# A residual stream kept feature by feature in a two-layer encoder: output projection and row norms

## The chip, the cores and the metric

One core of a Trainium2 chip runs the whole program in one launch. The metric is the device time of that launch in microseconds. A core has TensorE (matmuls, with its own weight loads), VectorE, ScalarE, GpSimd and SyncE (SP, which here issues all DMAs), and 16 DMA engines between DRAM and the on-chip memories SBUF (128 partitions) and PSUM (where matmuls write).

## The reference, cut to what matters

Two request groups, a prompt of 1024 rows and a sample of 512, go through two layers with the same weights; a row has 1024 features.

```
h = rms_norm(x, norm_g[l])                       # x / sqrt(mean(x^2) + 1e-6) * g, row by row
u = h @ w_in[l]                                  # 1024 x 3840: branches and gate
mkv = rms_norm(mem, mem_norm_g[l]) @ w_mem_kv[l] # 256 memory rows per group
layer 0: short gated conv | sliding-window attention | memory attention
layer 1: axial attention  | differential attention   | memory attention
x = x + (concat(branches) * silu(z)) @ w_out[l]  # 1280 x 1024
```

All is float32. The kernel writes each float32 factor of a large matmul as a high and a low part and adds three products: high x high, high x low, low x high.

## The kernel before, in words

Tokens go in halves of 512 (two for the prompt, `hf` 0 and 1, one for the sample). The projections take the contraction in 128 features at a time; activations for them lie in SBUF with the features on the partitions, in pairs of tiles [128, 2, 512] (ring `act`, 16 tiles). A weight chunk is 256 columns wide and comes in 4 pairs (`load_w`, line 204; 5 for the output projection): a DMA into `wraw`, ScalarE's cast to the high part `whi` (line 186), and a subtraction for the low part `wlo` (line 187) on VectorE or GpSimd in turns. `whi` and `wlo` have 7 tiles each.

`mm_a` (line 301) holds 128 tokens of activations stationary and moves 256 weight columns: the result has tokens on the partitions. `mm_b` (line 315) holds 128 weight columns stationary and moves 512 tokens: the result has features on the partitions. Queries, keys, values and, in this kernel, the output projection use `mm_a`; the gate and conv chunks use `mm_b`.

The residual `x` is kept row by row in DRAM (`x1`). `norm_steps` (line 234) norms 128 rows at a time: a load of [128, 1024], a square with a row sum on ScalarE, the power -0.5 on GpSimd (line 223), the scaling on VectorE (line 246), then 8 transposes by TensorE into PSUM (`hT`, line 253) and the multiplication by the gain on the way out (line 264). `put_act` splits the result into `act` tiles, `put_dram` stores it as `h`, from where `load_act` reads it later. The memory rows of both groups are normed twice, once for each layer's gain.

`out_proj` (line 887) adds the projection in PSUM (`po`) to the residual (`xr`, line 904) and stores it. It is called six times: two halves of the prompt and the sample, in both layers.

The order is written out at the end (lines 918 to 999): projections in chunks, with attention between them. Attention is marked urgent. `BG` holds steps that are worked off inside the projections (`between`, `bg`), `TAIL` and `STACK` the second half of a chunk's eviction, `ahead` loads what the next stage needs before the last chunk of this one. Every tile belongs to a ring with a fixed number of buffers (`BUF_TABLE`), and `in_order` makes each ring's tiles be taken in program order; a scheduler then places the instructions of every engine. Ring `bw` has 6 tiles of [128, 512] for evictions; ring `d` has two PSUM banks for the projections; ring `e` has 4 tiles of [128, 1024] for softmax.

Of the kernel before, what the change touches and what calls it, by code (L numbers as in the profile page):

```python
# [18 lines left out]
D = 1024  # L19
# [49 lines left out]
def trunk_kernel(ctx: ExitStack, tc: tile.TileContext, a: dict, dbg=None):  # L69
# [81 lines left out]
    def rope_table(nm, tag="xh"):  # L151
# [3 lines left out]
        cs = ring(sb, [128, 1024], F32, tag, "cs").rearrange("p (t a d) -> p t a d", t=8, a=2)  # L155
# [9 lines left out]
    for g, T in GROUPS.items():  # L165
# [16 lines left out]
    S["m", 1, "h"] = dr.tile([128, KT, 512], F32, name="h_m1")  # L182
# [51 lines left out]
    def norm_steps(rows, put, banks="x"):  # L234

        hh = {}

        def vec(t):
            x = ring(sb, [128, 1024], F32, "xh", "x")
            dma(out=x, in_=rows[t])  # L240
            sq = bw("sqx").bitcast(BF16)
            ss = small(1, "ss")
            nc.scalar.activation(out=sq, in_=x, func=ACTF.Square, accum_out=ss)
            rs = small(1, "rs")
            rstd(rs, ss, 1.0 / D, EPS)
            nc.vector.tensor_scalar(out=x, in0=x, scalar1=rs, scalar2=None, op0=ALU.mult)
            hh[t] = x

        def tr(t, q):
            ps = ring(psum, [128, 4, 128], F32, banks, "hT")  # L250
            for k in range(4):
                kk = 4 * q + k
                nc.tensor.transpose(ps[:, k, :], hh[t][:, kk * 128:(kk + 1) * 128], ident)
            put(t, q, ps)

        v = [lambda t=t: vec(t) for t in range(4)]
        x = [lambda t=t, q=q: tr(t, q) for t in range(4) for q in range(2)]
        return [v[0], v[1], v[2], x[0], x[1], v[3], x[2], x[3], x[4], x[5], x[6], x[7]]

    def new_h():  # L260
        return [[None, None] for _ in range(4)]

    def times_gain(out, ps, gain, q):
        nc.vector.tensor_tensor(
            out=out, in0=ps, in1=gain[:, 4 * q:4 * q + 4].unsqueeze(2).to_broadcast([128, 4, 128]), op=ALU.mult
        )

    def put_act(hs, gain):
        def put(t, q, ps):
            hg = bw("hg").rearrange("p (k t) -> p k t", k=4)  # L270
            times_gain(hg, ps, gain, q)
            for i in range(2):
                if t == 0:
                    hs[2 * q + i][:] = [ring(sb, [128, 2, 512], F32R, "act", f"h{j}") for j in range(2)]
                hi, lo = hs[2 * q + i]
                sl = slice(t * 128, (t + 1) * 128)
                src = hg[:, 2 * i:2 * i + 2, :]
                nc.scalar.copy(out=hi[:, :, sl], in_=src)
                (nc.gpsimd if i else nc.vector).tensor_tensor(out=lo[:, :, sl], in0=src, in1=f32(hi[:, :, sl]), op=ALU.subtract)
        return put  # L280

    def put_dram(dst, tok0, gain):
        def put(t, q, ps):
            ht = ring(sb, [128, 512], F32, "stk", "ht").rearrange("p (k t) -> p k t", k=4)
            times_gain(ht, ps, gain, q)
            dma(out=dst[:, 4 * q:4 * q + 4, tok0 + t * 128:tok0 + (t + 1) * 128], in_=ht)
        return put
# [157 lines left out]
    def load_h(g, l):  # L445
        return [load_half(g, l, hf) for hf in range(GROUPS[g] // 512)]
# [664 lines left out]
```

## Time and profile before

| what | value |
|---|---|
| runs, us | 2143.18, 2148.21, 2146.79; median 2146.79 |
| profiled execution, us | 2149.06 |
| its span, us | 2147.3 |
| mean granted TensorE clock | 0.99 of 2.4 GHz |
| TensorE, its weight loads, VectorE, ScalarE, GpSimd busy | 96%, 88%, 73%, 52%, 45% |
| DMA | 363.68 MB |

The span runs from the first to the last instruction of the profiled execution. The profile prints for a group of instructions its line, engine, operation, tiles, shapes and count, the busy time and the mean of one, and the idle time of the engine before them with what ended it. Matmuls overlap, so the distance between their starts, not their duration, tells what one costs.

### The profile page before, as it was taken

The page shows a single profiled execution, that of the slowest core. Times are in us where ns is not written, and L with a number is a line of the kernel's source. Part 1 is how long each engine was busy: PE and PEld are TensorE (multiplying, and loading weights), DVE is VectorE, ACT ScalarE, POOL GpSimd, SP SyncE. Part 2 cuts the span into 40 slices and gives each one's busy share as a digit, 9 for nine tenths or more (in the row PEclk, how much of TensorE's full clock was granted, in tenths as well). Part 3 has the DMA queues.
Part 4 walks back from the last instruction along what each step waited for, and adds up shares of the span by engine and source line. Part 5 has one row for each costly group of instructions (what it writes and reads, how often), then busy time and mean ns, then how long its engine had stood idle before and what let it go on. Part 6 is the DMA issues. An engine that isn't in the chain of part 4 may idle for free. (4 is left out here: it accounts for less than half of the span.)

```text
span 2147.3 us, 40432 instructions
## 1 busy us (share of the span) xinstructions
PE 2060.5 (96%) x14056; PEld 1893.4 (88%) x14056; DVE 1560.8 (73%) x3340; ACT 1116.5 (52%) x2634; POOL 968.0 (45%) x994
## 2 busy tenths in 40 slices
PE   6999999999999999999999999987998999999999
PEld 6988888889999999999998888876997898999999
DVE  8769877655446697976989987877769977775642
ACT  5445434453334566666666554546556556654541
POOL 6744511342224564643754653432355675643331
PEclk9999999999999999999999999998999999999999
DMA  6686743336777533434437566466566566677753
GB/s 231 192 242 179 225 113 89 112 104 224 249 234 226 168 105 93 119 116 118 111 116 215 166 182 178 123 181 172 157 202 202 162 189 190 177 216 216 227 155 99
DMA packets 321051, 363.68 MB, mean 169 GB/s; under 512 B 27984, under 2 KB 227408, under 8 KB 320848
## 3 DMA queue, kind: packets, MB, share of 16 engines
q1 hardware_dynamic: 320848, 361.11, 56.7%
q8 instruction: 111, 1.82, 0.4%
q14 instruction: 92, 0.75, 0.1%
HBM read 261.38 MB, written 99.61 MB: 168 GB/s over the span
## 5 line engine op out<-in xcount | busy, mean ns | idle before, releaser
L187 POOL TENSOR_TENSOR wlo<-wraw,whi 128x512 fp32r<-128x512 f32 x182 | 247.1, 1358 | 362.0 <-ACT whi L186 332.6
L681 ACT ACTIVATE e<-s,nm 128x512 f32<-128x512 f32 (+1 forms) x416 | 264.9, 640 | 231.6 <-DVE nm L679 149.5
L186 ACT CAST whi<-wraw 128x512 fp32r<-128x512 f32 x388 | 236.3, 621 | 235.9 <-PE po L311 71.8
L679 DVE TENSOR_REDUCE nm<-s 128x1 f32<-128x512 f32 (+1 forms) x368 | 249.7, 682 | 35.6 <-PE s L584 33.7
L590 ACT CAST pthi<-pT 128x512 fp32r<-128x512 f32 x352 | 201.1, 587 | 141.6 <-PE pT L669 61.5
L591 DVE TENSOR_TENSOR ptlo<-pT,pthi 128x512 fp32r<-128x512 f32 x352 | 238.0, 683 | 46.1 <-ACT pthi L590 44.5
L309 PE MATMUL po<-whi,ahi 128*128 128x256 f32 x896 | 255.6, 286 | 2.7 <-DVE xr L904 1.4
L310 PE MATMUL po<-wlo,ahi 128*128 128x256 f32 x896 | 255.3, 285 | 0.8 <-DVE wlo L187 0.8
L311 PE MATMUL po<-whi,alo 128*128 128x256 f32 x896 | 254.1, 285 | 0.1
L187 DVE TENSOR_TENSOR wlo<-wraw,whi 128x512 fp32r<-128x512 f32 x206 | 170.1, 826 | 78.3 <-ACT whi L186 76.3
L309 PE MATMUL pa<-whi,ahi 128*128 128x256 f32 x768 | 219.4, 286 | 1.3 <-ACT raw L381 0.7
L310 PE MATMUL pa<-wlo,ahi 128*128 128x256 f32 x768 | 220.2, 287 | 0.0
L311 PE MATMUL pa<-whi,alo 128*128 128x256 f32 x768 | 219.3, 286 | 0.2 <-DVE alo L187 0.2
L223 POOL TENSOR_TENSOR rs<-ss,mhalf 128x8 f32<-128x8 f32 (+2 forms) x108 | 142.2, 1317 | 145.7 <-DVE ss L219 121.1
L583 PE MATMUL s<-k,qhh 128*128 128x512 f32 (+2 forms) x512 | 194.4, 385 | 12.9 <-ACT e L681 7.7
L584 PE MATMUL s<-k,qll 128*128 128x512 f32 (+2 forms) x512 | 183.6, 364 | 2.0 <-DMA qll<-st_p1dq 1.3
L309 PEld LDWEIGHTS po<-whi,ahi 128*128 128x128 f32 x896 | 172.2, 192 | 4.9 <-ACT ahi L186 1.9
L310 PEld LDWEIGHTS po<-wlo,ahi 128*128 128x128 f32 x896 | 172.3, 192 | 2.5 <-DVE wlo L187 1.2
L311 PEld LDWEIGHTS po<-whi,alo 128*128 128x128 f32 x896 | 171.9, 192 | 1.4 <-DVE alo L187 0.3
L324 PE MATMUL pb<-h,whi 128*128 128x512 f32 x432 | 171.6, 397 | 0.0
L325 PE MATMUL pb<-h,wlo 128*128 128x512 f32 x432 | 170.7, 396 | 0.0
L323 PE MATMUL pb<-h,whi 128*128 128x512 f32 x432 | 170.3, 394 | 0.0
(170 smaller groups left out, 6043.5 us busy)
## 6 DMA issues: line engine op xcount, KB each, us to landing
wraw<-in_w_in_dram SPq DMA_DIRECT2D x252, 256.0 KB, 3.1
wraw<-in_w_out_dram SPq DMA_DIRECT2D x120, 256.0 KB, 3.6
alo<-y_p SPq DMA_DIRECT2D x20, 512.0 KB, 5.3
zg_p<-z SPq DMA_DIRECT2D x32, 256.0 KB, 2.8
k<-st_p1dk SPq DMA_DIRECT2D x14, 512.0 KB, 4.3
v<-dv_p SPq DMA_DIRECT2D x14, 512.0 KB, 5.0
zg<-zg_p SPq DMA_DIRECT2D x48, 128.0 KB, 2.7
y_p<-yo SPq DMA_DIRECT2D x48, 128.0 KB, 2.6
```

The costliest lines, as they stand in the source:

```text
L186: nc.scalar.copy(out=out_hi, in_=src)
L187: lo_eng.tensor_tensor(out=out_lo, in0=src, in1=f32(out_hi), op=ALU.subtract)
L309: nc.tensor.matmul(out=out, lhsT=h, rhs=wh, start=(k == 0), stop=False)
L310: nc.tensor.matmul(out=out, lhsT=h, rhs=wl, start=False, stop=False)
L311: nc.tensor.matmul(out=out, lhsT=l_, rhs=wh, start=False, stop=(k == n - 1))
L324: nc.tensor.matmul(out=out, lhsT=wh, rhs=l_, start=False, stop=False)
L583: nc.tensor.matmul(out=out, lhsT=q2[0], rhs=k, start=True, stop=False)
L584: nc.tensor.matmul(out=out, lhsT=q2[1], rhs=k, start=False, stop=True)
L590: nc.scalar.copy(out=hi, in_=ps)
L591: nc.vector.tensor_tensor(out=lo, in0=ps, in1=f32(hi), op=ALU.subtract)
L679: nc.vector.tensor_reduce(out=nm, in_=s, axis=AXL.X, op=ALU.max, negate=True)
L681: nc.scalar.activation(out=e[:, j, :], in_=s[:, j, :], func=ACTF.Exp, bias=nm[:, j:j + 1], accum_out=su[:, j:j + 1],)
```

## The change

The host hands `x` and the memory over with the features on the partitions ([128, 8, T]), and the outputs leave in that form. `out_proj` uses `mm_b`: 128 output features from stationary weights, 512 tokens moving. The row norm adds squares over the eight feature tiles (`sum_sq`), sums over the partitions with a matmul against `ones`, and spreads the scale of each token over all partitions with a transpose (`row_scale`). The scale `rs` is stored in DRAM in place of `h`; `load_half` loads `x` and `rs`, multiplies, and splits. The sums for layer 1 are made inside the layer-0 `out_proj`. Ring `xh` goes; `ym`, `ac` and `rs` come.

```diff
-    "act": 16, "whi": 7, "wlo": 7, "wraw": 3, "xh": 3, "stk": 5, "bw": 6, ...
+    "act": 16, "whi": 7, "wlo": 7, "wraw": 3, "ym": 2, "ac": 1, "rs": 2, "stk": 5, "bw": 6, ...
-        S[g, "x1"] = dr.tile([T, D], F32, name=f"x1_{g}")
+        S[g, "x1"] = dr.tile([128, KT, T], F32, name=f"x1_{g}")
         for l in range(2):
-            S[g, l, "h"] = dr.tile([128, KT, T], F32, name=f"h_{g}{l}")
+            S[g, l, "rs"] = dr.tile([128, T], F32, name=f"rs_{g}{l}")
-    def norm_steps(rows, put, banks="x"):
...
+    def sum_sq(acc, src, k, eng):
+        if k == 0:
+            nc.scalar.activation(out=acc, in_=src, func=ACTF.Square)
+            return
+        sq = bw("sqx")[:, 0:src.free_size()]
...
+        nc.scalar.activation(out=sq, in_=src, func=ACTF.Square)
+        eng.tensor_tensor(out=acc, in0=acc, in1=sq, op=ALU.add)
+    def row_scale(acc, dst):
+        m, n = acc.shape[1:]
+        nt = n // 128
+        ps = ring(psum, [128, 512], F32, "x", "ssx")
+        for t in range(nt):
+            for i in range(m):
+                nc.tensor.matmul(
+                    out=ps[:, 2 * t:2 * t + 2], lhsT=acc[:, i, t * 128:(t + 1) * 128], rhs=ones,
+                    start=(i == 0), stop=(i == m - 1),
+                )
+        s8 = small(2 * nt, "s8")
+        nc.vector.tensor_scalar(out=s8, in0=ps[:, 0:2 * nt], scalar1=1.0 / D, scalar2=EPS, op0=ALU.mult, op1=ALU.add)
+        nc.gpsimd.tensor_tensor(out=s8, in0=s8, in1=mhalf[:, 0:2 * nt], op=ALU.pow)
+        rb = bw("rbx")
+        pr = ring(psum, [128, 512], F32, "x", "rbx")
+        for t in range(nt):
+            sl = slice(t * 128, (t + 1) * 128)
+            nc.vector.tensor_scalar(
+                out=rb[:, sl], in0=ident, scalar1=0.0, scalar2=s8[:, 2 * t:2 * t + 1], op0=ALU.mult, op1=ALU.add
+            )
+            nc.tensor.transpose(pr[:, sl], rb[:, sl], ident)
+        r = ring(sb, [128, 512], F32, "rs", "rs")[:, 0:n]
+        nc.scalar.copy(out=r, in_=pr[:, 0:n])
+        if dst is not None:
+            dma(out=dst, in_=r)
+        return r
+    def scaled(hl, i, c, x, gain, r):
+        nc.vector.scalar_tensor_tensor(out=x, in0=x, scalar=gain, in1=r, op0=ALU.mult, op1=ALU.mult)
+        split(hl[0][:, i, c], hl[1][:, i, c], x, nc.gpsimd if i else nc.vector)
+    def norm_steps(xs, hs, c, gain, dst=None, eng=None):   # 4 x sum_sq, row_scale, 4 x scaled; sums on GpSimd unless eng
...
+    def stat_steps(src, dst):                              # loads into ring e, 4 x sum_sq, row_scale
...
+    def load_half(src, rs, gain):
+        r = ring(sb, [128, 512], F32, "rs", "rs")
+        dma(out=r, in_=rs)
+        hs = [pair_tiles() for _ in range(4)]
+        for k in range(KT):
+            x = bw("xs")
+            dma(out=x, in_=src[:, k, :])
+            scaled(hs[k // 2], k % 2, slice(0, 512), x, gain[:, k:k + 1], r)
+        return hs
     def out_proj(g, l, hf, ys, ahead=None):
...
+        acc = ring(sb, [128, 512], F32, "ac", "acc") if l == 0 else None
...
-            for tp in range(2):
-                ps = ring(psum, [128, 2, 256], F32, "d", "po")
-                for t in range(2):
-                    tt = 2 * tp + t
-                    mm_a(ps[:, t, :], ys, slice(tt * 128, (tt + 1) * 128), w, lambda: between(0))
...
+            for c in range(2):
+                k = 2 * ci + c
+                ps = ring(psum, [128, 512], F32, "d", "po")
+                mm_b(ps, ys, w, slice(c * 128, (c + 1) * 128), lambda: between(0))
+                xr = bw("xr")
+                dma(out=xr, in_=src[:, k, :])
                 nc.vector.tensor_tensor(out=xr, in0=ps, in1=xr, op=ALU.add)
+                dma(out=dst[:, k, tsl], in_=xr)
+                if l == 0:
+                    sum_sq(acc, xr, k, nc.gpsimd)
+        if l == 0:
+            row_scale(acc.unsqueeze(1), S[g, 1, "rs"][:, tsl])
-    BG.extend(norm_steps(mem_rows(), put_act(hm, gm0), "s"))
-    bg(12)
-    BG.extend(norm_steps(rows_of(a["x_p"]), put_act(hp[0], g0), "s"))
-    bg(3)
-    rope_table("swa_k", "e")
-    rope_table("swa_q", "e")
+    ca, cb, cc = slice(0, 256), slice(256, 512), slice(0, 512)
+    xm = [stage("e") for _ in range(4)]
+    norm_load(xm, a["mem"], ca)
+    wm = load_w(a["w_mem_kv"][0, 0], range(4))
+    norm_load(xm, a["mem"], cb)
+    BG.extend(norm_steps(xm, hm, ca, gm0, S["m", "rs"][:, ca], nc.vector))
+    BG.extend(norm_steps(xm, hm, cb, gm0, S["m", "rs"][:, cb], nc.vector))
+    bg(18)
+    xp = [stage(x) for x in "kkkv"]
+    norm_load(xp, x_of("p", 0), cc)
     load_constants()
-    mem_kv(0, hm)
-    bg(12)
-    BG.extend(norm_steps(rows_of(a["x_p"], 1), put_act(hp[1], g0), "s"))
-    BG.extend(norm_steps(rows_of(a["x_s"]), put_dram(S["s", 0, "h"], 0, g0)))
-    BG.extend(norm_steps(mem_rows(), put_dram(S["m", 1, "h"], 0, gm1)))
+    rope_table("swa_k", "v")
+    rope_table("swa_q", "v")
+    BG.extend(norm_steps(xp, hp[0], cc, g0))
+    mem_kv(0, hm, w0=wm)
+    bg(len(BG))
+    xp = [stage("e") for _ in range(4)]
+    norm_load(xp, x_of("p", 0, 1), cc)
+    BG.extend(norm_steps(xp, hp[1], cc, g0))
+    BG.extend(stat_steps(x_of("s", 0), S["s", 0, "rs"]))
...
-    BG.extend(norm_steps(rows_of(S["p", "x1"]), put_dram(S["p", 1, "h"], 0, g1)))
-    bg(3)
-    out_proj("p", 0, 1, nxt["y1"], ahead("m", lambda: load_act(S["m", 1, "h"], range(4))))
-    BG.extend(norm_steps(rows_of(S["p", "x1"], 1), put_dram(S["p", 1, "h"], 512, g1)))
-    bg(3)
+    out_proj("p", 0, 1, nxt["y1"], ahead("m", lambda: load_half(a["mem"], S["m", "rs"], gm1)))
...
-    hs = [new_h()]
-    BG.extend(norm_steps(rows_of(S["s", "x1"]), put_act(hs[0], g1)))
-    bg(3)
+    hs = load_h("s", 1)
```

`load_h` and `load_hf` call `load_half`: six times in all (memory for layer 1, two prompt halves for layer 1, the sample for layer 0, the second prompt half again, the sample for layer 1).

## Rows read from the trace of the kernel before

**Rows 1.** The page, part 1: busy us, share of the span, instructions.
```profile
PE 2060.5 (96%) x14056; PEld 1893.4 (88%) x14056; DVE 1560.8 (73%) x3340; ACT 1116.5 (52%) x2634; POOL 968.0 (45%) x994
```
**Rows 2.** Stretches: us, busy by engine (x instructions), granted clock, DMA share, GB/s.
```profile
0.00:100.00 100.00, 79.24 (x602) 76.14 (x603) 80.55 (x136) 55.15 (x128) 68.13 (x77) 0.98 0.66 212
...
300.00:400.00 100.00, 100.00 (x483) 83.41 (x482) 73.03 (x186) 39.01 (x99) 21.86 (x21) 1.00 0.32 94
...
1400.00:1500.00 100.00, 82.28 (x430) 65.97 (x429) 76.92 (x194) 56.13 (x152) 25.24 (x34) 0.91 0.63 182
...
580.00:590.00 10.00, 8.63 (x74) 8.43 (x72) 7.58 (x12) 3.46 (x7) 2.48 (x2) 1.00 1.07 382
```
**Rows 3.** Timeline of TensorE in the last output projection: start us, us; 24 steps apart.
```profile
2100.06 0.28 PE L309 MATMUL po<-whi,ahi 128*128 128x256 f32 x1
...
2102.93 0.28 PE L309 MATMUL po<-whi,ym 128*128 128x256 f32 x1
```
**Rows 4.** Timeline of TensorE in a gate chunk; 12 steps apart.
```profile
299.94 0.39 PE L323 MATMUL pb<-h,whi 128*128 128x512 f32 x1
...
302.67 0.39 PE L323 MATMUL pb<-h,whi 128*128 128x512 f32 x1
```
**Rows 5.** Groups of TensorE: busy us, mean ns | idle before.
```profile
L309 PE MATMUL po<-whi,ahi 128*128 128x256 f32 x896 | 255.6, 286 | 2.7 <-DVE xr L904 1.4 <-ACT ahi L186 1.3
...
L253 PE MATMUL hT<-ident_r,x 128*128 128x128 f32 x256 | 41.9, 294 | 18.5 <-DVE ss L219 7.3 <-DVE hg L264 6.4 <-DVE ht L264 4.8
...
L309 PE MATMUL po<-whi,ym 128*128 128x256 f32 x64 | 18.7, 294 | 2.8 <-ACT ym L186 2.8
```
**Rows 6.** Timeline of TensorE around four row-norm transposes.
```profile
45.44 0.28 PE L309 MATMUL pm<-whi,h 128*128 128x256 f32 x1
45.56 0.60 PE L253 MATMUL hT<-ident_r,x 128*128 128x128 f32 x4
...
46.12 0.28 PE L311 MATMUL pm<-whi,h 128*128 128x256 f32 x1
```
**Rows 7.** Timeline of TensorE around two matmuls against `ones` (four records).
```profile
2060.13 0.28 PE L310 MATMUL po<-wlo,ahi 128*128 128x256 f32 x1
2060.26 0.50 PE L809 MATMUL ss<-ones,osq 128*128 128x2 f32 x4
...
2060.82 0.28 PE L309 MATMUL po<-whi,ahi 128*128 128x256 f32 x1
```
**Rows 8.** What TensorE waited for: us in total, times, longest us.
```profile
PE pT L669 <- DVE e L660: 8.5, 3, 5.6
...
PE hT L253 <- DVE ss L219: 7.3, 1, 7.3
PE hT L253 <- DVE hg L264: 6.4, 6, 3.7
PE hT L253 <- DVE ht L264: 4.8, 4, 1.7
```
**Rows 9.** Groups of VectorE.
```profile
L187 DVE TENSOR_TENSOR wlo<-wraw,whi 128x512 fp32r<-128x512 f32 x206 | 170.1, 826 | 78.3 <-ACT whi L186 76.3 <-DMA qll<-st_p1q 1.1 <-PE pb L325 0.3
...
L246 DVE TENSOR_SCALAR x<-x,rs 128x1024 f32<-128x1024 f32 x32 | 34.1, 1064 | 9.7 <-POOL rs L223 9.6
...
L264 DVE TENSOR_TENSOR ht<-hT,gains 128x512 f32<-128x512 f32 x32 | 21.8, 683 | 6.7 <-PE hT L253 6.6
```
**Rows 10.** Groups of GpSimd.
```profile
L187 POOL TENSOR_TENSOR wlo<-wraw,whi 128x512 fp32r<-128x512 f32 x182 | 247.1, 1358 | 362.0 <-ACT whi L186 332.6 <-PE s L584 15.9 <-PE po L311 4.5
...
L816 POOL TENSOR_TENSOR s<-s,mhalf 128x4 f32<-128x4 f32 x24 | 25.1, 1046 | 31.7 <-DVE s L813 28.1 <-DVE su L657 2.6 <-DVE sk L698 0.9
```
**Rows 11.** Groups of ScalarE.
```profile
L383 ACT ACTIVATE sq<-raw 128x512 f32<-128x512 f32 (+1 forms) x76 | 45.6, 600 | 1.5
```
**Rows 12.** Tile `xr`: its DMAs, from issue to landing.
```profile
DMA to landing us min/median/max: 2.1/3.7/7.6
```

More of the change, by code (lines that the diff above doesn't have):

```diff
@@ L232, in bg @@
                     BG.pop(0)()
-    def norm_steps(rows, put, banks="x"):
[L236 to L258, printed above, removed]
@@ L260, in new_h @@
-    def new_h():
[L261 to L271, printed above, removed]
-            for i in range(2):
[L273 to L287, printed above, removed]
+    def sum_sq(acc, src, k, eng):
[3 more added lines that the diff above has]
+        sq = bw("sqx")[:, 0:src.free_size()]
+        if len(src.shape) == 3:
+            sq = sq.rearrange("p (k t) -> p k t", k=src.shape[1])
+        nc.scalar.activation(out=sq, in_=src, func=ACTF.Square)
+        eng.tensor_tensor(out=acc, in0=acc, in1=sq, op=ALU.add)
@@ new lines, in scaled, with pair_tiles, stage @@
+    def scaled(hl, i, c, x, gain, r):
+        nc.vector.scalar_tensor_tensor(out=x, in0=x, scalar=gain, in1=r, op0=ALU.mult, op1=ALU.mult)
+        split(hl[0][:, i, c], hl[1][:, i, c], x, nc.gpsimd if i else nc.vector)
+    def new_h():
+        return [None] * 4
+    def pair_tiles():
+        return tuple(ring(sb, [128, 2, 512], F32R, "act", nm) for nm in ("hhi", "hlo"))
+    def stage(tag):
+        return ring(sb, [128, 1024], F32R if tag in "kv" else F32, tag, "xs").rearrange("p (k t) -> p k t", k=2)
@@ new lines, in norm_load, with sq, end, put @@
+    def norm_load(xs, src, c):
+        for kp in range(4):
+            dma(out=xs[kp][:, :, c], in_=src[:, 2 * kp:2 * kp + 2, c])
+    def norm_steps(xs, hs, c, gain, dst=None, eng=None):
+        st = {}
+        eng = eng or nc.gpsimd
+        n = c.stop - c.start
+        m = 512 // n
+        def sq(kp):
+            x = f32(xs[kp][:, :, c])
+            if kp == 0:
+                st["a"] = ring(sb, [128, 512], F32, "ac", "acc").rearrange("p (m n) -> p m n", m=m)
+            for i in range(0, 2, m):
+                sum_sq(st["a"], x[:, i:i + m, :], 2 * kp + i, eng)
+        def end():
+            st["r"] = row_scale(st["a"], dst)
+        def put(kp):
+            if hs[kp] is None:
+                hs[kp] = pair_tiles()
+            for i in range(2):
+                scaled(hs[kp], i, c, f32(xs[kp][:, i, c]), gain[:, 2 * kp + i:2 * kp + i + 1], st["r"])
+        return [lambda kp=kp: sq(kp) for kp in range(4)] + [end] + [lambda kp=kp: put(kp) for kp in range(4)]
@@ L555, in mem_kv @@
                 ahead()
-            w = load_w(a["w_mem_kv"][l, ci], range(4))
+            w = w0 if w0 and ci == 0 else load_w(a["w_mem_kv"][l, ci], range(4))
             for gi, g in enumerate("ps"):
@@ L994, in trunk_kernel @@
     diff("s", 3)
-    ym = [ring(sb, [128, 2, 512], F32R, "xh", f"ym{i}") for i in range(2)]
+    ym = [ring(sb, [128, 2, 512], F32R, "ym", f"ym{i}") for i in range(2)]
     mem_attn("s", 1, ys=ym)
```

56 lines of the change are left out of this document (30 added, 26 removed), and 2 rows, old and new, of the table BUF_TABLE.

## The prediction

> **What bounds the kernel now.** Read the engine shares first: TensorE is busy for 2060.5 of 2147.3 us, 96%, VectorE for 73%, GpSimd for 45% [rows 1]. A busy TensorE by itself proves little, so look at the stretches next: 79 of the first 100 us are busy and 82 of the 100 from 1400, where the granted clock is 0.91 in the mean, part of it at 1.2 GHz; from 300 to 400, as in most stretches, TensorE hardly stops [rows 2]. The idle time is 2147.3 - 2060.5 = 86.8 us, a quarter of it (20.8 us) in the first 100 us. So the kernel is a TensorE stream with a few holes. What takes matmul time out of the stream shortens the span one for one; what only moves work between VectorE, ScalarE and GpSimd counts where it opens or closes a hole.
>
> **Output projection: 2880 matmuls become 1440.** Lines 309, 310 and 311 each run 896 + 64 = 960 times into `po`, 256 columns each [rows 5]. The new form has 6 calls x 4 chunks x 2 halves x 30 = 1440 matmuls of 512 columns: the same columns, half the instructions and weight loads. What counts is the distance from start to start, not the duration that the page prints (286 ns, which overlaps the next one). In the bare stretch near the end, 24 steps take 2102.93 - 2100.06 = 2.87 us, 0.1196 us each [rows 3]. The form to come exists already, in the gate chunks: 12 steps take 302.67 - 299.94 = 2.73 us, 0.2275 us each [rows 4]. One wide matmul for two narrow ones saves 0.2392 - 0.2275 = 0.0117 us, over 1440: **-16.8 us**, give or take 3 (0.002 us of reading error in each spacing). All of it lies on TensorE in stages where it is continuously busy, so I count it whole.
>
> On this the Trainium skill (TensorE: Matmul & The Clock Gate, Back-to-back issue gap) has another rule: a warm matmul costs N/2.4 ns plus about 2.5 ns, so a halved count would save only 2.5 ns each, 3.6 us in all, and my sum would end 13 us later. The rows show 13 ns above N/2.4 at 256 columns and 14 ns at 512, so the fixed part is larger here, and I stay with the rows.
>
> **Row norms: the transposes go.** All 256 `hT` transposes disappear [rows 5]. Four of them inside a matmul stream put off the second matmul behind them: from 45.44 to 46.12 is 0.68 us, where two plain steps are 0.24, so 0.44 us a group [rows 6]; 64 groups make 28.2 us. The first four groups run before anything else could, so 60 count: **-26.4 us**.
>
> In their place come eight row scales (two on the memory halves, two for the prompt, one for the sample, three after the layer-0 projections): 32 two-column matmuls against `ones` and 28 transposes. The differential attention does the same, and there two such matmuls (four records) put off the stream from 0.24 to 2060.82 - 2060.13 = 0.69, so 0.45 us [rows 7]. That is 16 x 0.45 + 7 x 0.44 = **+10.3 us**; in the prologue some lies in idle time, so 6 to 10.3; I take the upper end. TensorE's work changes by -16.8 - 26.4 + 10.3 = **-33 us**.
>
> **The holes.** Transposes waited for their eviction or their norm for 7.3 + 6.4 + 4.8 = 18.5 us [rows 8]. The 7.3 is the kernel's start and is replaced by another start: loads, four squares on ScalarE, sums on VectorE, a row scale, then a multiply. From durations (600 ns for a square [rows 11], 0.68 to 0.83 us for a VectorE pass of 512 [rows 9]) I get the first useful matmul at 13 to 14 us and a feed of about 1 us per 128 features. Before, the first stood at 15.6 us behind the same DMA wait, so the prologue neither gains nor loses more than 5 us. The other 11.2 us go. Against them stand new holes, at two places.
>
> First, the second prompt half. Its four stages sit in ring `e`, behind the memory values of the layer-0 memory projection, so two of them load only when that projection ends. From there: 3.7 us of landing [rows 12], about four remaining squares and sums at 1.36 us on GpSimd [rows 10] (5.5 us), a row scale of some 3.5 us, and the first scaled feature 2 us later: 15 us. TensorE has 96 matmuls of 0.12 us on the first half, 11.5 us, and then eats features as they come at about 1 us each where it wants one in 0.36. I take 6 us, bounds 0 (the scheduler loads earlier) and 12.
>
> Second, the hand-over from layer 0. The scale leaves through DRAM and comes back: residual add 0.69, square 0.60, sum 1.36, two-column matmuls 0.9, scale arithmetic and four spreads 1.4 (each under half of a 0.68 us pass), power 1.05, transposes 0.44, copy 0.6, store and load 3.7 each at the median, multiply, cast and subtract 2.1, together near 17 us [rows 6, 7, 9 to 12]. Before, the rows themselves made that trip, 3.7 + 3.7 and about 5 us of norm and transposes, 12 to 13 us. The chain is some 4 us longer. Behind the load of the scale on SP's queue wait that half's remaining loads and the next weights; seven weight pairs are held, 1.75 chunks of 11.5 us, so 17 us is just covered. For the prompt the second layer's memory projection (192 matmuls, 23 us) lies between, for the sample the differential attention. What is late next if this fails is `bw`: `load_half` takes eight of its tiles in order from a ring of six, and the evictions of the next chunk queue behind them. I take 5 us over the six loads, bounds 0 and 45.
>
> Holes: -11 + 6 + 5 = **0**, bounds -16 and +46.
>
> **What is off the path.** VectorE loses the 1024-wide scaling (34 us), both gain multiplies (21.8 us and its twin of the same count) and about 50 us of splits [rows 9]; it gains 80 multiplies, 40 subtracts and 28 spreads, about 105 us: net some -20. GpSimd gains 42 sums and 40 subtracts, mostly at 1.36 us, about +105, and loses about 45: 968 becomes near 1030, 48% of the span. ScalarE is even. Neither bounds. DMA loses 32 reads of 512 KB, 8 MB of stored `h` and 10 MB read back, 34 MB, and gains 8 MB for the sums, 13.5 for the six loads and 2 of stored scales: 11 MB less of 364. In the 10 us from 580, with the DMA share at 1.07, TensorE has a hole of 1.4 us [rows 2]; part of the 11 us above is of this kind, and I count no more for it.
>
> The Trainium skill (SBUF — State Buffer, Who interferes with whom) speaks against the change: a VectorE instruction with two SBUF inputs and a GpSimd instruction that reads SBUF exclude each other for the whole instruction. The trace agrees in kind: subtracts with two SBUF inputs average 826 ns on VectorE, and the gain multiply, which reads PSUM, 683 ns for the same size [rows 9]. At that 0.14 us each the 120 new such passes cost VectorE 17 us off the path. If every one waited out a whole GpSimd pass of 1.36 us it would be 163 us: VectorE at 79%, still under TensorE; it could only work through the hand-overs of the third rival.
>
> **The sum.** -33 + 0 on 2149.1 us, the profiled execution (1.8 us of it outside the span), gives 2116. That execution is 2.3 us above the median of the runs, 2146.79, so the forecast is **2114 us**.
>
> **Rivals.**
> 1. *The holes go too.* If the second half loads in time, the bw ring does not bite and the lighter DMA closes holes between 500 and 700 us: -33 - 16, and up to 10 us more from the prologue: 2088 to 2103, middle 2096. For it: VectorE and DMA have less to do. Against it: the largest single wait, 8.5 us for the softmax's scaling [rows 8], is touched by nothing. Chance 0.22.
> 2. *The projection saves nothing*, because a weight switch costs as much after 512 columns once interleaved with attention. Then -33 + 16.8 = -16 is left: 2131, in a range of 2127 to 2136. The Trainium skill's gap rule (the section named above) gives 2127 and has its chance here. Rows 4 are an interleaved stage, which speaks against it. Chance 0.12.
> 3. *The hand-overs stall: slower.* Mechanism: the in-order `bw` ring. While the eight tiles of `load_half` wait for the scale, the evictions of the following chunk get no buffer, both `d` banks fill and TensorE stops. Its price is the wait past what the two banks hold: up to 15 us at each of the three loads whose scale has just been made or whose buffers come late (prompt second half, its reload, sample), 12 us in the prologue, and a cold clock of 1.2 GHz for some microseconds after each. It decides when the holes grow by more than 33 us in net; at the bound of 46 the time is 2147 - 33 + 46 = 2160. For it: five evictions share six buffers. Against it: attention, which does not use `bw`, is urgent and fills TensorE in two of the three places. Chance 0.17.
> 4. *Washed out*: holes of about 28 to 36 us, time within 0.2% of 2146.8. Chance 0.07.
>
> **How the numbers follow.** Forecast (2103 to 2127): 0.42; rivals 0.22, 0.12, 0.17, 0.07. About 0.2%, 4.3 us, can be told from no change here. Faster: 0.42 + 0.22 + 0.12 = 0.76; same 0.07; slower 0.17. The range from 2088 to 2150 leaves out most of rival 3 and the far end of rival 1; the likeliest case alone spans 2103 to 2127.
>
> **What would show it.** Right: `po` at 0.2275 us a step with half the instructions; TensorE busy near 2028 us; no `hT`; idle TensorE time still 80 to 95 us; GpSimd near 1030. Wrong: `po` steps at 0.24; a hole above 10 us at the second prompt half or after each layer-0 projection with VectorE multiplies or DMA as the releaser; evictions that wait for `bw` while TensorE stands. A time above 2150 would mean the third rival; under 2090 that the idle time, not the matmuls, was the larger prize.

## The result, and the profile after

The changed kernel takes **2234.99 us** (median; 2233.89 to 2241.95) against 2147.5 us: a ratio of 1.0418, interval 1.0392 to 1.0444, 4.2% slower. Forecast were 2114 us and a range up to 2150; the sign was wrong too.

First the page's part 1 and its clock row, which stand against [rows 1], and then four stretches in the columns of [rows 2].

```profile
PE 2075.5 (93%) x12452; PEld 1826.2 (82%) x12452; DVE 1569.0 (70%) x3302; ACT 1118.6 (50%) x2610; POOL 1051.2 (47%) x1020
...
PEclk9699999999999999999999999998989999999979
```
```profile
0.00:100.00 100.00, 54.28 (x338) 50.25 (x338) 58.28 (x94) 43.11 (x84) 62.02 (x50) 0.84 0.49 158
100.00:200.00 100.00, 80.55 (x516) 74.48 (x517) 56.42 (x95) 33.24 (x71) 65.72 (x54) 0.89 0.69 212
300.00:400.00 100.00, 100.00 (x478) 82.69 (x477) 68.68 (x185) 40.07 (x106) 21.19 (x21) 1.00 0.37 106
1400.00:1500.00 100.00, 92.24 (x436) 75.05 (x435) 79.20 (x172) 51.00 (x119) 40.38 (x35) 0.95 0.51 156
```

TensorE executes 1604 matmuls fewer and is busy 15 us *longer*. 14 us of its busy time come from a slower step of the 512-column matmuls: the run `e7_sbuf_order` below undoes that and is busy for 2061.6 us at nearly the same clock (0.968). The mean granted clock fell from 0.99 to 0.966, and the idle time grew from 87 to 158 us. The first stretch holds 54 us of TensorE work where it held 79. No engine has become full: VectorE and GpSimd stand in the first 100 us at 58 and 62.

What TensorE waited for (columns as in [rows 8]):

```profile
PE pa L365 <- DVE hlo L187: 20.4, 3, 10.9
PE rbT L877 <- DVE rb L873: 11.0, 5, 2.8
PE pm L363 <- ACT hhi L186: 10.4, 3, 6.3
PE ssx L253 <- DVE acc L243: 9.2, 2, 8.5
PE rbx L267 <- DVE rbx L264: 8.7, 3, 3.7
...
PE pb L377 <- ACT raw L435: 8.2, 1, 8.2
```

Four of the first five are tiles of the new norm (`hlo`, `hhi`, `acc`, `rbx`). To see where time is lost I read the start of the same matmul in both traces (where a stage is "done", and for keys, its last matmul):

```
start of this matmul, us           before    after   difference
first memory projection done         55.7     61.9      +6.2
keys, first prompt half              70.7     86.9     +16.2
keys, second prompt half             84.8    125.5     +40.7
first output projection begins      503.9    544.0     +40.1
layer-0 projections (prompt) done   626.2    657.1     +30.9
layer-1 memory projection done      656.4    690.5     +34.1
first layer-1 keys, both halves     683.0    724.7     +41.7
sample's output projection begins  1434.5   1490.0     +55.5
last prompt projection begins      1915.2   1959.5     +44.3
last prompt projection done        2074.7   2107.5     +32.8
last matmul                        2143.1   2229.0     +85.9
```

Two steps stand out: 41 us in the first 125 us, and 53 us behind the last prompt projection, where 68.4 us had become 121.5. In between TensorE gains in the projections and loses at each hand-over and on each wide step.

### The profile page after: what moved, and what is told of

The parts are those of the page before. It is cut to its first block, busy times and chain, and to the rows that moved or that the text cites. A ratio compares the mean times of both kernels' runs of the same rounds, so it can differ in the third digit from the quotient of the medians.

```text
span 2233.2 us, 37197 instructions
## 1 busy us (share of the span) xinstructions
PE 2075.5 (93%) x12452; PEld 1826.2 (82%) x12452; DVE 1569.0 (70%) x3302; ACT 1118.6 (50%) x2610; POOL 1051.2 (47%) x1020
## 3 DMA queue, kind: packets, MB, share of 16 engines
q8 instruction: 99, 1.62, 0.3%
## 5 line engine op out<-in xcount | busy, mean ns | idle before, releaser
L365 PE MATMUL pa<-whi,hlo 128*128 128x256 f32 x1344 | 388.5, 289 | 21.3 <-DVE hlo L187 20.4
L363 PE MATMUL pa<-whi,hhi 128*128 128x256 f32 x1344 | 388.8, 289 | 6.5 <-ACT raw L435 2.7
L364 PE MATMUL pa<-wlo,hhi 128*128 128x256 f32 x1344 | 388.3, 289 | 0.0
L186 ACT CAST whi<-wraw 128x512 fp32r<-128x512 f32 x388 | 237.9, 621 | 259.0 <-PE po L378 68.6
L377 PE MATMUL pb<-hhi,whi 128*128 128x512 f32 x768 | 308.1, 401 | 8.2 <-ACT raw L435 8.2
L379 PE MATMUL pb<-hhi,wlo 128*128 128x512 f32 x768 | 308.6, 402 | 0.0
L378 PE MATMUL pb<-hlo,whi 128*128 128x512 f32 x768 | 307.1, 400 | 0.0
L365 PEld LDWEIGHTS pa<-whi,hlo 128*128 128x128 f32 x1344 | 259.1, 193 | 27.5 <-DVE hlo L187 21.4
L363 PEld LDWEIGHTS pa<-whi,hhi 128*128 128x128 f32 x1344 | 259.8, 193 | 13.7 <-ACT raw L435 3.1
L364 PEld LDWEIGHTS pa<-wlo,hhi 128*128 128x128 f32 x1344 | 259.8, 193 | 4.8
L377 PE MATMUL po<-ahi,whi 128*128 128x512 f32 x448 | 178.5, 400 | 5.4 <-ACT ahi L186 2.6
```

The costliest lines, as they stand in the source:

```text
L186: nc.scalar.copy(out=out_hi, in_=src)
L363: nc.tensor.matmul(out=out, lhsT=h, rhs=wh, start=(k == 0), stop=False)
L364: nc.tensor.matmul(out=out, lhsT=h, rhs=wl, start=False, stop=False)
L365: nc.tensor.matmul(out=out, lhsT=l_, rhs=wh, start=False, stop=(k == n - 1))
L377: nc.tensor.matmul(out=out, lhsT=wh, rhs=h, start=(k == 0), stop=False)
L378: nc.tensor.matmul(out=out, lhsT=wh, rhs=l_, start=False, stop=False)
```

## The experiments

All ratios are to the kernel before, run beside. Where nothing else is said, the edit is made in the changed kernel.

**The two parts apart.** `e1_wide_only` is the kernel before with only the wide output projection (the residual is then read and stored in contiguous stretches):

```diff
...
-                for t in range(2):
...
-                    mm_a(ps[:, t, :], ys, slice(tt * 128, (tt + 1) * 128), w, lambda: between(0))
...
+                mm_b(ps, ys, w, slice(c * 128, (c + 1) * 128), lambda: between(0))
...
```

> The kernel before with the wide output projection alone (mm_b, 1440 matmuls of 512 columns); norms, transposes and the row-wise loads stay. Each half's residual is read and written as 128 contiguous stretches, so its values are not the reference's. Theory W (the wide form saves TensorE time and is harmless): 2130 to 2137 us, the last matmul about 68 us after the prompt's layer-1 projection ends. Theory A (with the wide form less attention is placed beside a projection, so attention is left over for the end): 2160 to 2200 us, over 100 us from the end of the prompt's layer-1 projection to the last matmul. Spacing of 512-column matmuls: 227 ns if it goes with this kernel's layout, 232 ns if it goes with the chip or with the run.

Measured: 2171.08 us, ratio 1.0116 (1.0099 to 1.0132).

`e2_narrow_only` keeps the new norms and the new form of the residual and makes the projection narrow again (`mm_a` twice for each PSUM tile).

> The changed kernel with the output projection back in the narrow form (2880 matmuls of 256 columns); the new norms and the new layout stay, the values are not the reference's. Theory A: the tail of 121 us goes back to about 70 and the time to 2185 to 2205 us, the prologue's loss of 40 us stays. Theory N (everything lost comes from the new norms and the hand-overs, the tail too): 2235 to 2255 us, 11 to 17 us more than the changed kernel.

Measured: 2215.12 us, 1.0321 (1.03 to 1.0341). The stretch at the end is short again (66.8 us) and the prologue's loss stays, as theory A has it, but the time is 10 us above its range. So the norms alone cost 69 us and the wide form alone 25, which add up to 94 where 88 were measured together. Each part loses by itself; no rival of the prediction had that.

**Why the wide form loses: attention is left for the end.** Counting the attention matmuls (scores, transposes, outputs) that TensorE has done when 10,400 of its 256-column units of projection are through (a 512-column matmul is two):

```
             scores  transposes  outputs   last prompt projection to last matmul, us
before          946        1316     1229    68.4
e1 wide         916        1260     1168   118.9
e2 narrow       946        1316     1229    66.8
after           912        1252     1164   121.5
e5 split        950        1320     1232    57.2
```

The stretch behind the last prompt projection, from its end to the end of the span, of the changed kernel, and then of the run `e5_split_moving` below; first the stretch as in [rows 2], then groups as in [rows 5]:

```profile
2108.00:2234.00 126.00, 99.38 (x438) 79.05 (x436) 48.74 (x95) 40.89 (x98) 26.51 (x36) 0.87 0.35 105
```
```profile
L635 PE MATMUL s<-k,qhh 128*128 128x256 f32 (+1 forms) x22 | 8.5, 394 | 0.5 <-ACT e L733 0.3
...
L848 PE MATMUL pT<-ident_r,e 128*128 128x128 f32 x32 | 6.7, 350 | 1.1 <-DVE yo L880 1.1
```
```profile
2148.00:2209.00 61.00, 56.91 (x480) 56.70 (x478) 17.26 (x23) 11.24 (x19) 7.72 (x6) 0.99 0.36 114
```

In the changed kernel scores, softmax and transposes still run there, one step waiting for the other, with only the sample's last projection to fill TensorE; it idles 27 us and its clock falls to 0.87 in the mean. The split run has the same projection there and next to no attention: 93% busy.

`e5_split_moving` asks whether it is the layout or the number of matmuls that puts attention late. Same stationary weights, same PSUM tile, two matmuls of 256 for one of 512:

```diff
+        for m in range(2):
+            t = slice(256 * m, 256 * m + 256)
...
+                nc.tensor.matmul(out=out[:, t], lhsT=wh, rhs=h, ...)
```

> The changed kernel with one edit: each of the output projection's 512-column matmuls is issued as two of 256 columns (the same weights stationary, the same PSUM tile, the same eviction by features). Theory A1 (granularity): what puts attention late is that the order has half as many, longer matmuls to place attention between; then the attention done by the time three quarters of the last projections stand (10400 of the 256-column units) returns from 912 score matmuls to about 946, the stretch behind the last prompt projection from 121 us to about 67, and TensorE pays 1440 x 12 ns = 17 us for the narrower steps: 2205 to 2222. Rival A2 (layout): stationary weights and features on the partitions themselves (the eviction, the way the residual tiles are held) put it late; then the stretch stays at about 120 us, and the time is 2235 to 2252.

Measured: 2216.78 us, 1.0324 (1.0302 to 1.0346); attention is back where it was. The granularity does it, not the layout: with half as many, longer matmuls the scheduler that writes the program order places less urgent attention beside the same projection work. By what rule it does so, and whether the attention would have been ready earlier, no run shows. The narrower steps cost back 6.5 us (the distances of the `po` matmuls add up to 349.2 us against 342.7), and attention that leaves the tail takes its time earlier, so the time falls by 18 us and not by the tail's 64.

The split also doubles the places at which background steps are taken. `e14_wide_slots` (the kernel before, all wide, with two such places for each matmul group) separates that:

```diff
-            if mid and k == n // 4:
+            if mid and k in (n // 4, n // 4 + n // 2):
```

> The run of the kernel before with all six output projections wide, with one addition: background steps are taken at two places of each wide matmul group, so that a chunk has four such places, as the narrow form has. Theory B: in the earlier wide runs the row norms that work beside the output projection got half as many places, and the rest came after it (layer-1 memory projection ended 10 us late); then it ends at 656 to 658 us again and the time is 2158 to 2165; the order of attention, which does not hang on these places, leaves the same 50 us too much behind the last prompt projection (tail 118). Rival: the places also set where attention goes; then the tail returns to 68 us and the time is 2130 to 2140.

Measured: 2171.32 us, 1.0113 (1.0093 to 1.0132), as without the places. The scores at 10,400 units are 916 again and the tail is 118 us, so the places don't set where attention goes, and the granularity stands. But the memory projection still ends at 666.8 us: theory B falls for these 10 us.

`e12_wide_p0` and `e15_p0_slots` make only the two calls of the prompt's layer 0 wide, where hardly any attention runs beside them; the second with the added places.

> The kernel before, row norms and all, with the wide output projection in the two calls of the prompt's layer 0 alone; in these two calls the residual is read and stored as contiguous blocks in place of rows, so values differ, the bytes are the same. Theory A1: 480 x 12 ns = 5.6 us less, attention at 10400 units at 940 score matmuls (946 before, 916 with all six wide), the stretch behind the last prompt projection 68 us: 2139 to 2144. Rival A3: the wide form costs by itself (the layer-1 memory projection ended 10 us later with all six wide): 2147 to 2156.

> The run of the kernel before with only the two calls of the prompt's layer 0 wide, again with two places for background steps in each wide group. Theory B: the 10 us at the layer-1 memory projection were the missing places; then it ends at 651 to 657 us and the time is 2139 to 2146. Rival A3: the wide form saves nothing in these calls for another reason; then 2147 to 2156.

Measured: 2156.23 us, 1.0044 (1.0027 to 1.0061), and 2155.98 us, 1.0041 (1.0027 to 1.0056). The tail stayed short, as the theory had it, but no 5.6 us came: the layer-1 memory projection begins as late as before (625.0 and 626.3 us against 626.3) and ends 7 to 8 us later. What TensorE waits for from 560 to 660 us in the first of the two:

```profile
PE hT L253 <- DVE ht L264: 6.8, 5, 3.1
PE hT L253 <- DVE x L246: 4.4, 1, 4.4
PE po L323 <- DVE xr L904: 2.3, 1, 2.3
```

TensorE waits there for the row norms that follow and for a residual add, 13.5 us in all; in the kernel before, the same stretch has 4.2 us for `ht` and 1.4 for `xr`. In these runs such a norm needs all eight pieces of its half, where in the kernel before the first 256 rows were whole one step earlier; I hold that for the reason, but did not test it. If it is, the loss belongs to the way these runs store the residual and not to the wide form. These two calls alone lose about 9 us, and `e1_wide_only`, whose memory projection ends 10 us late as well, has the same loss among its 25 us: the attention at the end then accounts for some 16. In the changed kernel, which has no such norm, the wide form costs 20 us (2235.0 against 2215.1 in `e2_narrow_only`).

**Why the norms lose, in part: VectorE and GpSimd exclude each other.** `e3_vector_norm` moves the norms' sums in the first stages and all low parts of scaled features from GpSimd to VectorE, the busier of the two:

```diff
-        split(hl[0][:, i, c], hl[1][:, i, c], x, nc.gpsimd if i else nc.vector)
+        split(hl[0][:, i, c], hl[1][:, i, c], x, nc.vector)
...
-        eng = eng or nc.gpsimd
+        eng = eng or nc.vector
```

> The changed kernel with the norms' sums and all low parts of the normed activations on VectorE instead of GpSimd. Theory X (VectorE passes with two SBUF inputs wait for GpSimd passes): the multiply falls from 1004 ns to 700 to 760, the prompt's second half is ready some 15 us earlier, the time falls by 10 to 25 us. Theory C (the length of the chain and its late start decide): VectorE has more to do in the same places, the time changes by less than 8 us or rises.

Measured: 2198.02 us, 1.0244 (1.0228 to 1.0259): 37 us back by giving VectorE *more* work. The second half's keys end at 110.1 us, 15 us earlier, as theory X has it; scaling (797 ns) and time lie outside its ranges. The gain is not all in the prologue: it is 18 us when the first output projection begins, 31 when the sample's begins and 37 at the end. `e10_lo_vector` makes only the first of the two edits:

> The changed kernel with one edit: the 40 low parts of scaled features that GpSimd makes are made by VectorE; GpSimd keeps its 42 sums of squares. It splits the 37 us that VectorE alone gave back. Theory X1: the low parts on GpSimd are the cost, because each shuts VectorE's two-input passes out and TensorE waits for them; then the second half's keys end at 112 to 117 us (125 in the changed kernel, 110 with both moved), the scaling by line 276 falls from 1004 ns to 800 to 850, and the time is 2200 to 2212. Rival X2: the sums are the cost (they come one behind the other at 1.35 us before the first scale is known); then 2220 to 2232.

Measured: 2206.31 us, 1.0264 (1.0246 to 1.0281); second half's keys at 115.5 us. Theory X1: 29 of the 37 us are the 40 low parts.

The page's part 1 of `e10_lo_vector` and of `e3_vector_norm`:

```profile
PE 2071.1 (94%) x12452; PEld 1821.6 (83%) x12452; DVE 1571.2 (71%) x3342; ACT 1119.4 (51%) x2610; POOL 999.4 (45%) x980
```
```profile
PE 2069.3 (94%) x12452; PEld 1822.2 (83%) x12452; DVE 1571.3 (72%) x3356; ACT 1120.3 (51%) x2610; POOL 979.8 (45%) x966
```

VectorE runs 40 and 54 passes more than in the changed kernel and is busy for the same time (1569.0 us there): what it took over it got back in shorter passes. The edits also replace GpSimd's longer passes (1.62 us for a low part) by shorter ones, and no run separates that; but in the changed kernel TensorE waits that a GpSimd low part ended are 3.1 us in all, those that a VectorE low part ended 26.9.

How that looks in the traces. First VectorE, then GpSimd, in the changed kernel at the layer-1 load (start us, us, engine, line, operation):

```profile
689.67 1.77 DVE L276 SCALAR_TENSOR_TENSOR xs<-xs,gains,rs 128x512 f32<-128x512 f32 x1
...
693.22 0.85 DVE L276 SCALAR_TENSOR_TENSOR xs<-xs,gains,rs 128x512 f32<-128x512 f32 x1
693.99 1.76 DVE L187 TENSOR_TENSOR wlo<-wraw,whi 128x512 fp32r<-128x512 f32 x1
```
```profile
689.16 1.73 POOL L187 TENSOR_TENSOR hlo<-xs,hhi 128x512 fp32r<-128x512 f32 x1
...
692.17 1.36 POOL L187 TENSOR_TENSOR hlo<-xs,hhi 128x512 fp32r<-128x512 f32 x1 [1.28 <-ACT hhi L186]
693.48 3.40 POOL L187 TENSOR_TENSOR wlo<-wraw,whi 128x512 fp32r<-128x512 f32 x2
```

The pass that starts at 689.67, while GpSimd runs until 690.89, takes 1.77 us and ends 0.55 us after GpSimd's; the one at 693.22, which meets only the end of a GpSimd pass, takes 0.85; the one at 693.99, again behind a running one, 1.76. The groups show it as a mean: of the changed kernel, and of `e3_vector_norm`.

```profile
L276 DVE SCALAR_TENSOR_TENSOR xs<-xs,gains,rs 128x512 f32<-128x512 f32 x64 | 61.8, 1004 | 13.9 <-DMA xs<-in_mem_dram 6.5 <-DMA rs<-rs_s 2.6 <-DMA rs<-rs_p 2.3
...
L187 DVE TENSOR_TENSOR hlo<-xs,hhi 128x512 fp32r<-128x512 f32 x32 | 34.3, 1082 | 0.1
```
```profile
L276 DVE SCALAR_TENSOR_TENSOR xs<-xs,gains,rs 128x512 f32<-128x512 f32 x64 | 49.1, 797 | 13.6 <-DMA xs<-in_mem_dram 5.0 <-DMA rs<-rs_p 2.6 <-DMA xs<-x_s 2.3
L187 DVE TENSOR_TENSOR hlo<-xs,hhi 128x512 fp32r<-128x512 f32 x64 | 46.1, 746 | 0.0
```

64 low parts on VectorE take 46 us; 32 of them beside GpSimd took 34. At the sharpest place the chain of scaling runs into GpSimd's preparation of two tables, where eight half-size passes take 9.95 us in the changed kernel and 6.36 in `e3_vector_norm`. This place is not the low parts' doing: in `e10_lo_vector`, whose sums stay on GpSimd, the same passes take 10.51 us.

```profile
29.21 9.95 DVE L276 SCALAR_TENSOR_TENSOR xs<-xs,gains,rs 128x256 f32<-128x256 f32 x8
```
```profile
30.72 6.36 DVE L276 SCALAR_TENSOR_TENSOR xs<-xs,gains,rs 128x256 f32<-128x256 f32 x8
```
```profile
27.87 10.51 DVE L276 SCALAR_TENSOR_TENSOR xs<-xs,gains,rs 128x256 f32<-128x256 f32 x8
```

This is the rule of the Trainium skill (SBUF — State Buffer, Who interferes with whom) that the prediction had cited, and the traces agree with it: the VectorE pass above that starts at 689.67 us waits until the GpSimd pass is over at 690.89.

**What else holds the prologue.** `e4_early_half` norms the second prompt half ahead of the memory projection:

> The changed kernel with the prompt's second half loaded and normed before the layer-0 memory projection is issued; the layer-0 memory values use ring stk instead of ring e, so that the stages are free. Theory C (late start): the hole before the second half's first key-value matmuls, 24 us wider than before the change, shrinks by 15 us or more, the time falls by 12 to 25 us. Theory X: the norm's passes crowd the same engines earlier and the hole moves ahead, less than 8 us gained.

Measured: 2246.24 us, 1.047 (1.0452 to 1.0487): 11 us worse, keys at 152 us. The late load is not the cost by itself. TensorE's longest wait there is at a row scale, for a sum of squares on GpSimd (4.5 us in the changed kernel):

```profile
PE ssx L253 <- POOL acc L243: 31.3, 1, 31.3
```

`e8_pe_sums` takes the sums off both engines: TensorE sums the squares with a matrix of 1/1024, which gives all partitions the mean; low parts on VectorE, projection split as in e5.

```diff
+                    nc.tensor.matmul(out=st["ps"], lhsT=mean, rhs=q[:, k, :], ...)
...
+            nc.scalar.activation(out=r, in_=st["ps"], func=ACTF.Ln, bias=epst)
+            nc.scalar.activation(out=r, in_=r, func=ACTF.Exp, scale=-0.5)
```

> The changed kernel with three edits: output projection in 256-column matmuls as in the split run; in the norms of the first stages every low part on VectorE, none on GpSimd; and there the squares are summed by TensorE, which is idle, with a 128 x 128 matrix of 1/1024 (all partitions receive the mean), followed by a logarithm and an exponential on ScalarE, so that the 28 adds, the 2-column matmuls, the powers, the spreads and transposes of the first four row scales go. Its projection ring also lies on PSUM banks 2 and 3. Theory X (VectorE with GpSimd beside it is what holds the first 110 us): the second prompt half's keys end near 95 us (changed 125, all on VectorE 110, before 85), and with the split's gain the time is 2150 to 2175. Rival: the prologue is held by the loads or by the order, then the keys end at 105 or later and the time is 2175 to 2200.

Measured: 2192.03 us, 1.0217 (1.0195 to 1.0238), keys at 106.7 us. VectorE works 68.6 of the first 120 us there against 92.9 in the kernel before, which ends the same keys at 84.8: the total work of the vector engines no longer holds this stage. Theory X misses its place and its time; the rival, loads or order, has both. Part of the 25 us that e8 gains over e5 is not the norm's: its 512-column step is 227 ns and no longer 232 (see below).

Three more were built on it: `e9_sums_early` (the second half early, as in e4), `e11_hybrid` (e9 with the two layer-0 prompt calls wide) and `e13_sums_256` (e8 with the prompt normed in parts of 256 tokens, and with more background steps in a matmul group: five for three in the first projections, three for two in the memory projection).

> The sums run (norm sums by TensorE, low parts on VectorE, output projection in 256-column matmuls) with the second prompt half loaded and normed ahead of the layer-0 memory projection. Theory Y: with VectorE and GpSimd relieved, what holds the first 107 us is that the second half's tiles load late (TensorE works 2.0 of the 10 us from 80); then its keys end at 90 to 96 us (107 without this edit) and the time is 2176 to 2184. Rival C (crowding, as in the early run on the changed kernel, where this edit cost 11 us): VectorE is full from 10 to 60 us and the memory projection is held up instead; the keys end at 105 or later, 2190 to 2205.

> The run with the early second half, with the wide matmuls of 512 columns again in the two calls of the prompt's layer 0 alone (480 of 1440). Theory A1 (the wide form leaves attention over only where attention is running beside it, from the sample's layer 0 on): TensorE gains 480 x 12 ns = 5.6 us and the stretch behind the last prompt projection stays near 67 us: 4 to 8 us less than the run without it. Rival A3 (wide matmuls cost elsewhere as well): no gain or a loss.

> The sums run (second prompt half not moved) with the two prompt halves of the first stages normed in parts of 256 tokens instead of 512 (and one background step more per matmul group to keep up). Theory G: what is left of the prologue's loss is that 512 tokens must have all eight squares summed before the first of them can be scaled, where the kernel before norms 128 rows at a time and TensorE can take them at once; then the second half's keys end at 96 to 101 us (107 with parts of 512, 85 before) and the time is 2180 to 2187. Rival V: VectorE's and ScalarE's total work holds it; smaller parts add fixed costs (16 more passes each), and the keys end at 107 or later, 2190 to 2200.

Measured: 2186.69 (1.0176; 1.0159 to 1.0192), 2187.84 (1.0189; 1.0168 to 1.021) and 2184.93 us (1.0171; 1.0149 to 1.0194). The keys end at 116.4, 115.8 and 111.6 us: neither theory Y nor theory G is borne out by the place it names, although e9 and e13 are 5 to 7 us faster over the whole; the gain lies in later stages, and I have no cause for it. The hybrid gains nothing over e9. What holds the last 22 us of the prologue (e8's keys at 106.7 us against 84.8) is open.

**Where the tiles lie.** A 512-column step takes 227 ns in the kernel before and in e1, and 232 to 233 in the changed kernel, also in the gate chunks, which nobody touched. Twelve steps of the changed kernel, as in [rows 4]:

```profile
300.01 0.39 PE L378 MATMUL pb<-hlo,whi 128*128 128x512 f32 x1
...
302.80 0.39 PE L378 MATMUL pb<-hlo,whi 128*128 128x512 f32 x1
```

> The changed kernel with only the PSUM banks of its rings moved to where the kernel before has them: the projection ring d on banks 2 and 3 instead of 1 and 2, scores on 0 and 1, the small ring on 4. Theory P: the banks set the step of a 512-column matmul, 227 ns before and 232 ns after; then the gate chunks step at 227 ns and the time falls by about 4000 x 5 ns = 20 us, to 2210 to 2220. Rival S: the addresses in SBUF set it; then 232 ns and 2230 to 2240. Rival N: neither does, the same.

> The changed kernel with only the SBUF rings in another order of addresses: activations below the weights, as in the kernel before (activations from 33856, weights from 115776; changed kernel: weights from 37952, activations from 91584, in bytes of a partition). Theory S: the order of addresses sets the step of a 512-column matmul; then the gate chunks step at 227 ns and the time is 2210 to 2220. Rival P: the PSUM banks set it; then 232 ns and 2230 to 2240.

Both only take the first buffers of the rings in another order, with small writes at the start, for instance:

```diff
+    for tag, w in (("bw", 512), ("act", 1024), ("e", 1024), ("wlo", 512), ("whi", 512), ("wraw", 512)):
+        t = sb.tile([128, w], F32, tag=tag, name=f"first_{tag}", bufs=BUFS[tag])
+        nc.vector.memset(t[:, 0:2], 0.0)
```

PSUM order: 2234.09 us, 1.0405 (1.0389 to 1.042), still 0.2325 us a step. SBUF order: 2221.05 us, 1.0351 (1.0334 to 1.0368), and twelve steps of it are

```profile
301.61 0.39 PE L380 MATMUL pb<-hhi,whi 128*128 128x512 f32 x1
...
304.33 0.39 PE L380 MATMUL pb<-hhi,whi 128*128 128x512 f32 x1
```

2.72 us, 0.2267 each. SBUF addresses it is: 13 to 14 us, the time 1 us above theory S's range. Which relation of addresses is open. The runs e2 to e5 and e10 step at 232 ns like the changed kernel, so their comparison with it is free of this effect; e8, e9, e11 and e13 step at 227 ns, though nobody reordered their SBUF rings. By the share of 512-column matmuls that e8 still has (2304 of 3744), I estimate 8 to 9 of its 25 us as this effect.

## Why the prediction was wrong, point by point

- **"All of it lies on TensorE in stages where it is continuously busy, so I count it whole" (the wide projection, -16.8 us)** failed. The saving itself was right: the sum of the `po` distances without gaps fell from 354.8 us to 337.7 in e1, 17.1 us, near the 16.8 from [rows 3, 4] and far from the 3.6 that the prediction weighed beside them; in the changed kernel, with its slower step, it fell to 342.7. The step that failed is counting it whole. A saved microsecond of projection counts only while attention can take its place, and with the wide form attention was left for the end: the tail grew by 50.5 us in e1, which became 25 us slower. The prediction treated the order as fixed; the change rewrote it.
- **"The prologue neither gains nor loses more than 5 us"** failed: the first half's keys were 16 us late. **"I take 6 us, bounds 0 ... and 12" (second prompt half)** failed as well: from the first to the second half's keys 38.6 us instead of 14.1, 24.5 more. The estimate took VectorE's passes at 0.68 to 0.83 us and GpSimd's at 1.36, the means of the kernel before [rows 9, 10], and counted a pipeline at about 1 us a feature. The scaling alone took 1.00 us a pass, the low parts 1.08 on VectorE and 1.62 on GpSimd. From 60 to 130 us TensorE's largest wait is for them:

```profile
PE pa L365 <- DVE hlo L187: 18.2, 2, 10.9
```

- **"What is off the path"** is where the mechanism stood and was dismissed. The exclusion was priced at 17 us, at worst 163, and set off against VectorE's share of the whole span. The share said nothing of the places where TensorE waits for the scaling and its low parts. Moving the work off GpSimd gave back 37 us, 29 of it by the low parts.
- **Transposes gone, -26.4; row scales, +10.3**: near in size. The `hT` distances were 28.7 us (28.2 by the prediction's own reckoning for all 64 groups) and the two new groups take 13.3.
- **Holes of the transposes, -11**: they went, but TensorE's new waits above are larger. **Hand-overs, 5 us, bounds 0 and 45**: the largest are 6.7 us between the prompt's last layer-0 matmul and the memory projection behind it (0.1 before), 7.5 more from that projection's end to the end of the first layer-1 keys, and 8.2 at the sample's load; inside the bounds, but more than four times the value taken. The releasers of the first two are mostly `hhi` and `hlo`. At the sample's load it is the third rival's own mechanism, once: the scale lands, VectorE scales six features in a row, and the eviction `raw` gets its `bw` tile only when a low part has released one, while TensorE stands for 8.2 us.

```profile
1650.92 6.08 DVE L276 SCALAR_TENSOR_TENSOR xs<-xs,gains,rs 128x512 f32<-128x512 f32 x6 [2.64 <-DMA rs<-rs_s]
```
```profile
1659.04 0.58 ACT L435 COPY raw<-pa 128x512 f32<-128x512 f32 x1 [1.00 <-DVE hlo L187]
```

That is below the 15 us a place that it named. It had the sign, but it is a small part of the loss, and at 2160 its end was 75 us too low.
- **Not foreseen**: the 5 ns of each 512-column step from the placement of the tiles, 13 to 14 us, and the clock. With its two levels, 1.2 and 2.4 GHz, a mean of 0.966 over 2233 us is 152 us at the lower one, a mean of 0.99 over 2147 us is 43: some 110 us more. By the means of the stretches shown above, about 87 of the 152 us lie in the first 200 us and in the tail, where TensorE has its holes. What the lower clock cost in time no run separates.
- **What would show it**: `po` steps at 232 ns instead of 227.5, TensorE busy for 2075 instead of 2028 us and GpSimd at 1051 (near 1030 forecast). A time above 2150 "would mean the third rival": the time came, but the rival's mechanism was seen for 8.2 us, about a tenth of the loss.

The account of the 88 us: 69 by the norms and 25 by the wide projection, each alone, 6 less because the parts overlap. Within the changed kernel, taking work off GpSimd gives back 37 us and the other placement 13 to 14, each measured alone. But these do not add up to an account of the 69: e8 has the low parts and the first sums off GpSimd, the narrow projection and the 227-ns step, and it is 25 us faster than e5, not 50, and still 44 us slower than the kernel before. Against that kernel e8 is 16 us late when the first output projection begins, 31 when the sample's layer-0 one begins and 41 when the last prompt projection begins; what holds these stages is open. No version that I ran beats the kernel before; the fastest with the new norm is e13, 1.7% slower.

## What to carry to other kernels

Price a matmul saved on a full TensorE together with the work that has to fill its place: where a scheduler interleaves urgent, latency-bound work, changing the size of the dense matmuls changes the interleaving, so count both kinds of work at the same mark of the trace and look at the stretch behind the last dense stage. Judge shared resources stage by stage: an average of 70% on VectorE hides a prologue in which TensorE waits 18 us for its passes, and there GpSimd beside it can cost more than it takes over.

## What the runs showed of the hardware

- A change of SBUF addresses alone moves the 512-column step from 0.2325 to 0.2267 us; the 256-column step stays at 119 to 120 ns in all kernels, and other PSUM banks for the rings change neither.
- Moving 40 two-input passes from GpSimd to VectorE leaves VectorE's busy time where it was (1569.0 and 1571.2 us), because its other two-input passes get shorter: the scaling falls from 1004 to 829 ns in the mean.
- In the prologue of e8 the squares' sums by TensorE (float32, 512 columns, granted clock 1.00) take 1.12 us for two in a row, and each table load before the logarithm costs ScalarE 1.28 us:

```profile
21.25 1.12 PE L312 MATMUL ssp<-sqx,mean 128*128 128x512 f32 x2 [1.20 <-ACT sqx L310]
```
```profile
L319 ACT ACT_TABLE_LOAD x4 | 5.1, 1283 | 0.1
```
